# Encoder trunk with two attention mixers: the amount of filler between attention rounds corrected in 28 of 218 rounds, filler allowed past four group ends, ten attention steps moved by a round or by some places

## The chip, the cores and the metric

One Trainium2 chip, one of its cores. The metric is device time in microseconds (us) of one execution of the whole program, the median over repeated runs. The core has five instruction queues that matter here: TensorE (PE, with PEld for its weight loads), VectorE (DVE), ScalarE (ACT), GpSimd (POOL), and SyncE (SP), which only issues DMA transfers.

## The reference

One transformer layer on 1,280 tokens of width 1,024 (1,024 of one request group, 256 of another), all in float32:

```python
n = _rms_norm(h, g_mix, NORM_EPS)
z = jnp.einsum('bsd,dc->bsc', n, w_in)
qa, ka, va, qb, kb, vb = jnp.split(z, cuts, axis=-1)
# mixer A: 4 heads, two softmax maps per head, distance penalty
sc = jnp.einsum('bqhcd,bkhcd->bhcqk', qb, k) * scale - slopes * dist
pr = jax.nn.softmax(sc, axis=-1)
out = jnp.einsum('bhqk,bkhe->bqhe', pr[:, :, 0] - lam * pr[:, :, 1], v)
# mixer B: 8 query heads on 2 key/value heads, normed and rotated q and k
ob = _gqa_attention(qb, kb, vb)
h = h + jnp.einsum('bsc,cd->bsd', jnp.concatenate([oa, ob], -1), w_out)
a = jax.nn.relu(jnp.einsum('bsd,df->bsf', _rms_norm(h, ...), w_ff1))
h = h + jnp.einsum('bsf,fd->bsd', a * a, w_ff2)
h = h + sigmoid(_rms_norm(h, ...) @ w_ple_gate) * (p @ w_ple_proj)
return _rms_norm(h, g_final, NORM_EPS)
```

The softmax is exact: the maximum over the keys is taken, then the exponential, then the division by the sum.

## The kernel before

Every float32 matrix product is made of three matmuls of rounded parts: high by high, high by low, low by high. So nearly every operand is split first: ACT copies it to the rounded type (the high part), and DVE or POOL subtracts that from the original (the low part).

**Stages.** Up to about 120 us the tokens are normed and projected to the B mixer's q, k, v and the A mixer's v. Then the A mixer's q and k follow, and the attention of all heads starts at about 197 us and runs to about 711 us, with other matmuls woven between its steps. Behind it come the rest of the output projection, the transposes of the normed tokens, the MLP (seven products in place of eight, from about 790 us), the gate and the last norm. The change touches the attention stage alone.

**Attention units.** A unit is one head (or one of the two heads of a B pair) on 256 queries, against 1,024 or 256 keys. There are 60 units, written X here as A0 to A3 and B4 to B7 with the number of the first 128-token block: "B7 at block 6, first head". Their work is cut into steps, and each step is put down for a *round* by `at(r, ph, fn)`: `r` is the round, `ph` the phase within it, `fn` records the instructions. The steps of a unit are:

- `qk`: the scores, four matmuls of 512 columns into the PSUM tile `sc` (two buffers), L671;
- `mx`: the row maximum on DVE, with the distance penalty for A (L684, 1,024 columns), without it for B (L688);
- `ex`: the exponential on ACT (L693 for A, L696 for B); for B it is what frees the `sc` buffer, for A `mx` is;
- `cb`: the division, on POOL, and for A the difference of the two maps on DVE (L706);
- `tr`, `hi`, `lo`: four transposes on PE into the PSUM tile `tr` (two buffers, L725), the high part `ph` on ACT (L731), the low part `pl` on DVE (L736), which frees the `tr` buffer;
- `av`: the product with the values, two matmuls with `ph` (four for A) and two with `pl` (L749), two rounds after the `tr`; at the end of an A unit the norm of its result (L763 to L783, with a matmul L768 of the squares `osq`).

A unit with 1,024 keys has four `tr` steps in four rounds, and the next unit's `tr` steps follow; its scores stand four to seven rounds earlier. There are 218 rounds, 0 to 217.

**Filler.** Between the phases of a round the loop takes work from a generator, `side_work`. It holds first the q and k projections of A heads 1 to 3 (`psa`, L284), then, once the input activations are no more needed, the output projection: a first half for all ten token tiles (channels 0, 1, 4, 5), then the second half. Each token tile has two groups of twelve 512-column matmuls, `pso`. The generator hands out three matmuls at a time and says what they cost in the planner's units (648 for three of 512 columns); at the end of a group it says 0.0. How much is taken is a debt, `owed`:

```python
owed += max((cost + lead) * (0.0 if r <= 6 else RATIO if r < LATE else RATIO2), LEAD.get(r, 0.0))
while owed > 0:
    d = next(side, None)
    if op_done and not WN[0]:
        w1_fetch(0, 1)
    norms()
    if not d:
        owed = 0.0
        break
    owed -= d
```

`cost` is the planned cost of the round's attention matmuls, and 500 more is added for each `av` step of the round; `RATIO` is 0.43, and 0.6 from round 160 on. So at a group's end the round takes nothing more, and what is left of the debt is dropped. The evacuation of a finished group is recorded at the next round's start. Some of the 0.0 stand for preparation alone: when the output projection opens, each of four of them splits one channel's weights (`ow`: ACT L914, POOL L915) after their DMA has landed.

What the rounds do not take is left to a loop behind the attention, which alternates the remaining `pso` groups with the token transposes `trn` (L1137).

**What sets the order.** The recorded order is a priority. A scheduler then lists each engine's instructions, so matmuls of one step can stand between those of another; each engine then runs its own list in order. The places below are shown as that final list.

Of the kernel before, what the change touches and what calls it, by code (L numbers as in the profile page):

```python
# [46 lines left out]
def encoder_kernel(ctx: ExitStack, tc: tile.TileContext, x, xT, pT, w_in, w_out, w_ff1, w_ff2, w_gate, w_proj,  # L47
                   g_mix, g_mlp, g_ple, g_subln, g_final, g_qn, g_kn, lams, rope, dist, y):
    nc = tc.nc
    pp2 = []  # L50
    LEAD = {4: 2000., 5: 2000., 6: 2000.}
    PRE = 14000
    Y = (0, 1, 1)
# [52 lines left out]
    dp = ctx.enter_context(tc.tile_pool(name="dram", bufs=1, space=DRAM))  # L106
# [462 lines left out]
    def flush():  # L569
        todo, deferred[:] = deferred[:], []  # L570
        for fn in todo:
            fn()
# [33 lines left out]
    rounds = collections.defaultdict(list)  # L606
    PH = {n: i for i, n in enumerate(("ld", "tr", "mx", "hi", "ex", "cb", "st", "lo", "qk", "fill", "av", "fin"))}

    def at(r, ph, fn):
        rounds[r].append((PH[ph], len(rounds[r]), fn))  # L610

    def mixed_out(r, ch, t0, get):

        st = {}

        def hi():
            st["hl"] = tl("ml")
            S.activation(st["hl"][:, 0], get(), AF.Copy)

        def lo():  # L620
            hl = st["hl"]
            G.tensor_tensor(hl[:, 1], get(), f(hl[:, 0]), op=ALU.subtract)
            dma(MD[ch][:, :, t0:t0 + 256], f(hl[:]))
            md_done[ch, t0] = True

        at(r, "fin", hi)
        at(r + 1, "fin", lo)

    def plan_unit(kind, idx, t0, c, b, shared):
# [26 lines left out]
        def values():  # L656
# [3 lines left out]
            st["v"] = vals[n]  # L660

        at(when[0] - 3, "ld", start)
        at(when[0], "st", values)

# [336 lines left out]
    def w1_fetch(p, i):  # L1001
        hl = slot(f"W{EARLY[p][i]}", [P, 2, 4, P], F32R, "w1")
        dma(f(hl[:]), wed[p, i])
        WN[p][i] = hl[:, 0], hl[:, 1]
# [47 lines left out]
    def norms():  # L1052
        nonlocal normed
        while normed < len(op_done):
            mlp_norm(op_done[normed])
            normed += 1
# [4 lines left out]
    owed = PRE  # L1061
    while owed > 0:
        d = next(side)
        flush()
        owed -= d
    owed = 0.0
    last = max(rounds)
    for r in range(min(rounds), last + 1):
        cost = 0.0
        todo = sorted(rounds[r], key=lambda q: q[:2])  # L1070
        for ph, _, fn in todo:
            if ph < PH["fill"]:
                cost += fn() or 0.0
        flush()
        lead = sum((fn_ph == PH["av"]) * LC for fn_ph, _, _ in todo)
        owed += max((cost + lead) * (0.0 if r <= 6 else RATIO if r < LATE else RATIO2), LEAD.get(r, 0.0))
        while owed > 0:
            d = next(side, None)
            if op_done and not WN[0]:
                w1_fetch(0, 1)  # L1080
            norms()
            if not d:
                owed = 0.0
                break
            owed -= d
        for ph, _, fn in todo:
            if ph >= PH["fill"]:
                fn()
# [788 lines left out]
```

## Time and profile before

| | |
|---|---|
| median of the runs | 1680.98 us (1680.25 to 1682.56, three runs) |
| the profiled execution | 1681.47 us |
| its span, first to last instruction | 1679.7 us |
| granted TensorE clock, mean over the span | 0.997 of full speed |
| matmuls in the span | 9,777 |

The profiled execution is 0.49 us over the median, and 1.8 us of it lie outside the span. In the rows below "idle before" is time in which the engine had nothing running ahead of that instruction, and the arrow names what it waited for.

### The profile page before, as it was taken

How to read it: one execution, taken by the hardware profiler on the slowest of the kernel's cores; microseconds unless marked ns; L12 is line 12 of the kernel's file. 1: busy time of each engine (PE TensorE's matmuls, PEld its weight loads, DVE VectorE, ACT ScalarE, POOL GpSimd, SP SyncE). 2: the span in 40 equal slices, each digit the busy share in tenths (PEclk: the TensorE clock that was granted, in tenths of full speed). 3: DMA queues.
4: the chain of work that ended last, by engine and by line, in shares of the span. 5: the costliest groups of instructions: out<-in, count | busy, mean ns of one | idle time of the engine just before them, and what ended most of it. 6: DMA issues, size and time to landing. Idle time of an engine off the chain costs nothing.

```text
span 1679.7 us, 27298 instructions
## 1 busy us (share of the span) xinstructions
PE 1638.0 (98%) x9777; PEld 1468.3 (87%) x9777; DVE 1207.8 (72%) x2130; ACT 882.4 (53%) x1717; POOL 668.8 (40%) x706
## 2 busy tenths in 40 slices
PE   8999999999899999999999999999999999999997
PEld 8999888888788888889999999999888888888885
DVE  7788588778788878668766666666664856855876
ACT  8544377776776667675333332333433435745534
POOL 1123455545654445333656556630533400003343
PEclk9999999999999999999999999999999999999998
DMA  9766853432963434396433434439776459980463
GB/s 313 238 216 230 250 154 108 132 108 94 261 185 122 138 91 130 109 309 203 158 123 130 159 129 137 135 126 390 239 228 201 159 188 358 334 290 15 158 212 107
DMA packets 205964, 309.22 MB, mean 184 GB/s; under 512 B 14714, under 2 KB 124932, under 8 KB 205828
## 3 DMA queue, kind: packets, MB, share of 16 engines
q1 hardware_dynamic: 203940, 301.96, 54.9%
q0 software_dynamic: 1600, 5.24, 1.0%
q8 instruction: 77, 1.26, 0.3%
q14 instruction: 59, 0.48, 0.1%
q10 hardware_dynamic: 288, 0.27, 0.0%
HBM read 200.45 MB, written 101.72 MB: 180 GB/s over the span
## 4 chain that ended last, share of the span: by engine, by line
PE 81%; DVE 6%; DMA 5%; issue 3%; ACT 3%; POOL 2%; SPq 1%; POOLq 0%; ACTq 0%; DVEq 0%
PE psa L284 6%; PE sc L671 6%; PE av L749 5%; PE psg L1696 4%; PE tr L725 4%; PE pso L284 4%; PE psb L284 3%; PE psv L284 2%; PE psp L176 1%; DMA xt<-in_x 1%; DVE pl L736 1%; DMA h_sb<-in_x 1%; PE f__15611 L176 1%; DVE mm L688 1%; DVE nlo L1232 1%
## 5 line engine op out<-in xcount | busy, mean ns | idle before, releaser
L671 PE MATMUL sc<-kt,qt 128*128 128x512 f32 (+1 forms) x576 | 156.2, 391 | 8.3 <-ACT p L696 6.0
L736 DVE TENSOR_TENSOR pl<-tr,ph 128x512 fp32r<-128x512 f32 x204 | 138.0, 684 | 32.1 <-ACT ph L731 30.5
L731 ACT ACTIVATE ph<-tr 128x512 fp32r<-128x512 f32 x204 | 119.8, 595 | 56.8 <-PE tr L725 50.1
L1411 DVE TENSOR_TENSOR ao<-ar,ao 128x1280 fp32r<-128x1280 f32 x56 | 96.6, 1726 | 68.3 <-ACT ao L1409 68.3
L1409 ACT ACTIVATE ao<-ar 128x1280 fp32r<-128x1280 f32 x56 | 71.0, 1270 | 128.7 <-PE f__14937 L176 31.6
L284 PE MATMUL pso<-ow,mt 128*128 128x512 f32 x480 | 119.3, 395 | 3.0 <-DVE osq L776 1.3
L671 PEld LDWEIGHTS sc<-kt,qt 128*128 128x128 f32 x576 | 98.7, 188 | 26.8 <-ACT p L696 7.5
L725 PE MATMUL tr<-ident,p 128*128 128x128 f32 x768 | 115.6, 273 | 6.4 <-DVE pl L736 5.7
L725 PEld LDWEIGHTS tr<-ident,p 128*128 128x128 f32 x768 | 91.3, 140 | 23.0 <-DVE pl L736 9.3
L1125 POOL TENSOR_SCALAR w1r<-w1r,gmlp 128x256 f32<-128x256 f32 x112 | 79.1, 724 | 67.3 <-DMA w1r<-in_w_ff 67.3
L284 PEld LDWEIGHTS pso<-ow,mt 128*128 128x128 f32 x480 | 87.4, 188 | 21.1 <-DVE osq L776 2.0
L749 PE MATMUL av<-ph,vt 128*128 128x256 f32 x544 | 101.7, 288 | 0.8 <-DVE osq L776 0.4
L1198 ACT ACTIVATE w<-w1s 128x512 fp32r<-128x512 f32 x56 | 35.2, 629 | 114.7 <-POOL w1s L1205 55.1
L710 POOL TENSOR_SCALAR p<-p,rl 128x1024 f32<-128x1024 f32 x64 | 74.9, 1171 | 50.8 <-DVE rl L708 47.4
L1696 PE MATMUL psg<-gbo,gao 128*128 128x512 f32 (+1 forms) x387 | 91.0, 385 | 0.0
L688 DVE TENSOR_REDUCE mm<-sc 128x1 f32<-128x1024 f32 (+1 forms) x80 | 84.2, 1056 | 8.9 <-PE sc L671 8.4
L749 PE MATMUL av<-pl,vt 128*128 128x256 f32 x408 | 89.1, 300 | 0.0
L1798 POOL TENSOR_TENSOR ra<-ra 128x512 f32<-128x512 f32 x5 | 7.1, 1429 | 204.9 <-DVE gao L1542 204.9
L749 PEld LDWEIGHTS av<-ph,vt 128*128 128x128 f32 x544 | 81.8, 188 | 6.3 <-DVE osq L776 1.0
L696 ACT ACTIVATE p<-sc,mm 128x1024 f32<-128x1024 f32 x64 | 71.3, 1115 | 25.4 <-DVE mm L688 16.7
L1696 PEld LDWEIGHTS psg<-gbo,gao 128*128 128x128 f32 x387 | 70.9, 188 | 14.6
L684 DVE CUSTOM_DVE_ANT_0 p<-sc,dist 128x1024 f32<-128x1024 f32 x64 | 77.6, 1218 | 7.8 <-PE sc L671 3.8
(1545 smaller groups left out, 4829.1 us busy)
## 6 DMA issues: line engine op xcount, KB each, us to landing
ar<-ad SPq DMA_DIRECT2D x56, 640.0 KB, 5.2
w2r<-in_w_ff SPq DMA_DIRECT2D x56, 512.0 KB, 4.9
qt<-qd SPq DMA_DIRECT2D x160, 128.0 KB, 3.0
ad<-q SPq DMA_DIRECT2D x64, 320.0 KB, 2.9
ad<-qs SPq DMA_DIRECT2D x48, 320.0 KB, 2.2
w1r<-in_w_ff SPq DMA_DIRECT2D x28, 512.0 KB, 4.2
md<-ml SPq DMA_DIRECT2D x40, 256.0 KB, 2.5
mt<-md SPq DMA_DIRECT2D x20, 512.0 KB, 6.0
```

What stands on the lines that cost most here:

```text
L284: PE.matmul(ps, a, b, start=i == 0, stop=i == n - 1)
L671: PE.matmul(ps[:, h0:h0 + n], shared["q"][:, cc, v, i * P:(i + 1) * P], kt[:, s0 + h0:s0 + h0 + n], start=v == 0, stop=v == 1)
L684: V.tensor_tensor_reduce(out=p[:, :sn], in0=ps[:, :sn], in1=dst_t[:, off:off + sn], scale=SLOPES[idx], scalar=3.0e38, op0=ALU.add, op1=ALU ...
L688: V.tensor_reduce(out=st["m", i][:, 0:1], in_=ps[:, :sn], axis=AX.X, op=ALU.max, negate=True)
L710: G.tensor_scalar(p[:, :sn], p[:, :sn], rl[:, 0:1], 1.0, op0=ALU.mult, op1=ALU.mult)
L725: PE.transpose(t[:, jj, i * P:(i + 1) * P], st["ws"][i][:, j * P:(j + 1) * P], ident)
L731: S.activation(ph, st["tr", j2], AF.Copy)
L736: V.tensor_tensor(pl, st["tr", j2], f(st["ph", j2][:]), op=ALU.subtract)
L749: PE.matmul(st["av"][:, :256], x_, y_, start=j2 == 0 and n == 0, stop=j2 == nj - 1 and n == len(pr) - 1)
L1125: G.tensor_scalar(raw[:, k], raw[:, k], gmlp[:, 4 * kh + k:4 * kh + k + 1], 1.0, op0=ALU.mult, op1=ALU.mult)
L1411: V.tensor_tensor(ao[:, 1], a, f(ao[:, 0]), op=ALU.subtract)
L1696: ends[:] = [PE.matmul(ps, a, w, start=n == 0, stop=n == len(pr) - 1)]
```

## The change

```diff
+    FIX = {49: -1320, 59: -660, 62: 660, 66: -660, 75: -660, 76: 330, 79: 660, 81: 2000, 82: 660, 83: -660,
+           84: 660, 104: -1000, 106: -1320, 109: -1000, 116: -660, 118: 660, 122: -660, 130: 660, 140: -660, 146: -330,
+           150: -330, 169: 1320, 173: -330, 174: -1320, 188: -660, 189: 660, 206: 660, 209: -660}
+    BRK = {43: 2, 106: 1, 191: 1, 205: 2}
+    MV = {50: (0, -10), 109: (1, 0), 264: (-1, 0), 637: (0, -2), 1178: (-1, 0), 1275: (1, 0), 1291: (0, 10), 1491: (-1, 0),
+          1546: (0, -2), 1681: (0, 2)}
+    n_at = itertools.count()
...
     def at(r, ph, fn):
-        rounds[r].append((PH[ph], len(rounds[r]), fn))
+        dr, dp = MV.get(next(n_at), (0, 0))
+        rounds[r + dr].append((PH[ph], len(rounds[r + dr]) + dp, fn))
...
         owed += max((cost + lead) * (0.0 if r <= 6 else RATIO if r < LATE else RATIO2), LEAD.get(r, 0.0))
+        owed += FIX.get(r, 0.0)
+        brk = BRK.get(r, 0)
         while owed > 0:
...
             if not d:
+                if d is not None and brk > 0:
+                    brk -= 1
+                    flush()
+                    continue
                 owed = 0.0
                 break
```

`FIX` adds to or takes from the debt of 28 rounds; 660 is about one portion of three 512-column matmuls. `BRK` lets four rounds go on past a group's end, one or two times. `MV` moves ten of the steps: by a round (first number) or by places within the phase (second).

Followed round by round, the tables do less than they list. In rounds 43, 106 and 205 the loop meets no group end (in 43 and 106 the debt is below zero), so only round 191 goes past one. The added debt of rounds 169 and 189 is dropped at a group end. The moves 50 and 264 leave every engine's list as it was, and move 109 only lets SP issue the four query loads of B4 at block 8 ahead of the four of B4 at block 2, some 200 us into the program. PE's list is the same up to its matmul 2,228 (at 321 us in the trace), and DVE's, ACT's and POOL's up to about the same time. From there on the amount of filler behind the old one runs like this: 648 to 1,944 units less through rounds 49 to 80, up to 1,944 more in rounds 81 to 101, then less again, 1,296 at round 109, 2,592 at 122, 3,888 at 148, 6,480 at 175, and 7,776 from round 197 on. So 36 `pso` matmuls (three groups) come behind the last `av` that stood before it. The opening of the output projection, which had rounds 103 to 107 without matmuls of filler, now has rounds 102 to 109 without any. Nothing is added or removed: 576 `psa`, 480 `pso` and all attention matmuls remain, as do all instructions of the other engines. SP issues the same transfers, and where its list differs one to four neighbours change places; the loads of the residual rows and of `mt`, which belong to the filler, fall some places later along with their groups.

Three places on PE, with what stood there and what stands there now. In all three, `tr` rows of four are one `tr` step; `pso` is filler.

The first is near the end of the attention, with the `tr` steps of B7 at block 6, first head (four) and A3 at block 6 (four). Before:

```order
L725 MATMUL tr<-ident,p 128x128 x4
L749 MATMUL av<-pl,vt_8146 128x256 x2
L725 MATMUL tr<-ident,p 128x128 x9
L284 MATMUL pso<-ow,mt 128x512 x12
L725 MATMUL tr<-ident,p 128x128 x7
```

Now:

```order
L733 MATMUL tr<-ident,p 128x128 x4
L757 MATMUL av<-pl,vt_8111 128x256 x2
L733 MATMUL tr<-ident,p 128x128 x4
L291 MATMUL pso<-ow,mt 128x512 x12
L733 MATMUL tr<-ident,p 128x128 x4
L776 MATMUL av<-osq,mean_m 128x256
L733 MATMUL tr<-ident,p 128x128
```

The first row is the second `tr` step of B7, and the nine held its third, its fourth and one matmul of A3's first. The filler group now stands between the third and the fourth. A little further on, A3's third and fourth `tr` steps stood right behind the `av` rows of B7; the list there was

```order
L768 MATMUL av<-osq,mean_m 128x256
L725 MATMUL tr<-ident,p 128x128 x8
L284 MATMUL pso<-ow,mt 128x512 x12
L725 MATMUL tr<-ident,p 128x128 x8
L749 MATMUL av<-ph,vt_8146 128x256 x4
```

and is now

```order
L757 MATMUL av<-pl,vt_6362 128x256 x2
L291 MATMUL pso<-ow,mt 128x512 x12
L733 MATMUL tr<-ident,p 128x128 x8
L291 MATMUL pso<-ow,mt 128x512 x12
L757 MATMUL av<-ph,vt_8111 128x256 x4
```

so that a filler group has come ahead of them.

The second place is in the B6 unit at block 2, first head: its second `tr` step, then its third and fourth together. Ahead of them stand two groups of scores of A2 at block 2; the score behind them is the first of B6 at block 4, and it takes the buffer of the first of those two. Before:

```order
L671 MATMUL sc<-kt,qt 128x512 x4
L749 MATMUL av<-ph,vt_6357 128x256 x2
L671 MATMUL sc<-kt,qt 128x512 x4
L725 MATMUL tr<-ident,p 128x128 x4
L749 MATMUL av<-pl,vt_6357 128x256 x2
L768 MATMUL av<-osq,mean_m 128x256
L725 MATMUL tr<-ident,p 128x128 x8
L671 MATMUL sc<-kt,qt 128x512 x4
L725 MATMUL tr<-ident,p 128x128 x4
L284 MATMUL pso<-ow,mt 128x512 x12
```

Now:

```order
L679 MATMUL sc<-kt,qt 128x512 x4
L733 MATMUL tr<-ident,p 128x128 x4
L757 MATMUL av<-pl,vt_6362 128x256 x2
L776 MATMUL av<-osq,mean_m 128x256
L679 MATMUL sc<-kt,qt 128x512 x4
L733 MATMUL tr<-ident,p 128x128 x8
L291 MATMUL pso<-ow,mt 128x512 x12
L679 MATMUL sc<-kt,qt 128x512 x4
```

The second A2 group has moved between the `tr` steps, and the filler group ahead of B6's score.

The third place is the last unit, B7 at block 6, second head: its third and fourth `tr` steps and the `av` that need them. Before:

```order
L725 MATMUL tr<-ident,p 128x128 x8
L768 MATMUL av<-osq,mean_m 128x256
L749 MATMUL av<-ph,vt_6357 128x256 x2
L749 MATMUL av<-pl,vt_6357 128x256 x2
L749 MATMUL av<-ph,vt_6357 128x256 x2
L749 MATMUL av<-pl,vt_6357 128x256 x2
L749 MATMUL av<-ph,vt_6357 128x256 x2
L749 MATMUL av<-pl,vt_6357 128x256 x2
L749 MATMUL av<-ph,vt_6357 128x256 x2
L749 MATMUL av<-pl,vt_6357 128x256 x2
```

Now, from the fourth `tr` step on:

```order
L733 MATMUL tr<-ident,p 128x128 x4
L757 MATMUL av<-pl,vt_6362 128x256 x2
L757 MATMUL av<-ph,vt_6362 128x256 x2
L757 MATMUL av<-pl,vt_6362 128x256 x2
L757 MATMUL av<-ph,vt_6362 128x256 x2
L757 MATMUL av<-pl,vt_6362 128x256 x2
L1151 MATMUL trn<-ident,h_sb 128x128 x4
```

The last two `av` rows need the `ph` and the `pl` of that fourth step. Seven rows lay between it and the first of them, and three lie there now.

## The prediction

> **What bounds the kernel now.** First the page's busy times, then the same by stage.
>
> ```profile
> span 1679.7 us, 27298 instructions
> PE 1638.0 (98%) x9777; PEld 1468.3 (87%) x9777; DVE 1207.8 (72%) x2130; ACT 882.4 (53%) x1717; POOL 668.8 (40%) x706
> ```
>
> ```profile
> core 0: us, PE busy (x) PEld busy (x) DVE busy (x) ACT busy (x) POOL busy (x), PEclk, DMA share, GB/s
> ...
> 120.00:320.00 200.00, 198.52 (x1273) 177.45 (x1272) 158.55 (x339) 118.48 (x257) 99.08 (x104) 1.00 0.60 182
> 320.00:720.00 400.00, 381.61 (x2365) 330.31 (x2365) 312.12 (x588) 278.27 (x582) 199.50 (x217) 1.00 0.46 136
> 720.00:790.00 70.00, 67.15 (x394) 60.62 (x393) 53.18 (x105) 45.05 (x90) 22.37 (x31) 1.00 0.80 262
> ```
>
> PE is the bound, and the change neither adds nor removes a matmul. So the time can change only by PE's idle time: 400 - 381.61 = 18.4 us in the stretch from 320 to 720 us, where the lists differ, and 2.9 us behind it. DVE has 312 us of work there, 78%: it is no bound on the average, but in a stretch of some microseconds it may be. Next, who is waited for there:
>
> ```profile
> line engine op names shapes xcount | busy us, mean ns | idle before us <-releasers
> L671 PE MATMUL sc<-kt,qt 128*128 128x512 f32 (+1 forms) x420 | 113.6, 391 | 8.3 <-ACT p L696 6.0 <-DVE mm L684 1.9
> L736 DVE TENSOR_TENSOR pl<-tr,ph 128x512 fp32r<-128x512 f32 x159 | 108.0, 685 | 27.8 <-ACT ph L731 26.5 <-PE av L768 0.3
> L731 ACT ACTIVATE ph<-tr 128x512 fp32r<-128x512 f32 x158 | 93.1, 595 | 46.2 <-PE tr L725 40.8 <-PE av L749 4.6
> L284 PE MATMUL pso<-ow,mt 128*128 128x512 f32 x357 | 90.0, 395 | 3.0 <-DVE osq L776 1.3 <-DVE o L797 0.7 <-ACT ow L914 0.5
> L725 PE MATMUL tr<-ident,p 128*128 128x128 f32 x592 | 88.6, 273 | 6.3 <-DVE pl L736 5.7 <-DVE rl L703 0.4
> L749 PE MATMUL av<-ph,vt 128*128 128x256 f32 x426 | 79.2, 287 | 0.8 <-DVE osq L776 0.4 <-ACT ph L731 0.2
> ```
>
> The idle time before PE's groups (8.3 + 3.0 + 6.3 + 0.8) makes up the 18.4 us. Almost all of it is a wait for a PSUM buffer: `sc` until ACT or DVE has read it, `tr` until `pl` is made. Both have two buffers. So what counts at each place is the **distance**: how much other PE work stands between the group that fills a buffer and the one that wants it back. PE's pace for that work, from the chain of waits:
>
> ```profile
> 418.79 1.86 PE sc L671 x8
> 421.36 0.44 PE tr L725 x4
> 501.44 1.88 PE av L749 x16
> 586.81 2.77 PE pso L284 x12
> ```
>
> A `tr` step is 0.44 us, a score group of four 0.93, a pair of `av` 0.235, a whole filler group 2.77. The single waits, from the timeline of PE:
>
> ```profile
> 369.97 0.66 PE L725 MATMUL tr<-ident,p 128*128 128x128 f32 x4 [0.75 <-DVE pl L736]
> 371.11 1.21 PE L671 MATMUL sc<-kt,qt 128*128 128x512 f32 x4 [0.48 <-DVE mm L684]
> 408.96 0.65 PE L725 MATMUL tr<-ident,p 128*128 128x128 f32 x4 [1.14 <-DVE pl L736]
> 446.50 1.20 PE L671 MATMUL sc<-kt,qt 128*128 128x512 f32 x4 [2.93 <-ACT p L696]
> 460.23 0.51 PE L284 MATMUL pso<-ow,mt 128*128 128x512 f32 x1 [0.54 <-ACT ow L914]
> 461.59 0.73 PE L284 MATMUL pso<-ow,mt 128*128 128x512 f32 x2 [0.42 <-POOL ow L915]
> 494.00 0.60 PE L725 MATMUL tr<-ident,p 128*128 128x128 f32 x4
> 495.23 0.66 PE L725 MATMUL tr<-ident,p 128*128 128x128 f32 x4 [0.63 <-DVE pl L736]
> 496.37 1.20 PE L671 MATMUL sc<-kt,qt 128*128 128x512 f32 x4 [0.48 <-DVE mm L684]
> 535.87 3.02 PE L284 MATMUL pso<-ow,mt 128*128 128x512 f32 x12 [0.66 <-DVE o L797]
> 622.06 3.06 PE L284 MATMUL pso<-ow,mt 128*128 128x512 f32 x12 [1.34 <-DVE osq L776]
> 643.62 1.19 PE L671 MATMUL sc<-kt,qt 128*128 128x512 f32 x4 [1.08 <-ACT p L696]
> 688.52 1.05 PE L725 MATMUL tr<-ident,p 128*128 128x128 f32 x5 [1.11 <-DVE pl L736]
> 696.77 1.45 PE L725 MATMUL tr<-ident,p 128*128 128x128 f32 x8 [0.77 <-DVE pl L736]
> ```
>
> **The change, part by part.** The sum is made against the profiled execution, 1681.47 us, which lies 0.49 us over the median.
>
> *The end, 686 to 699 us.* The fourth `tr` step of B7 wants the buffer of the second; between them stood a pair of `av` and the third step, 0.235 + 0.44 = 0.67 us. The trace shows what is needed there:
>
> ```profile
> 686.14 0.60 PE L725 MATMUL tr<-ident,p 128*128 128x128 f32 x4
> ```
>
> That is the second step; its PE time ends at 686.14 + 0.44 = 686.58, and the fourth starts at 688.52, 1.94 us later. Now a filler group stands between as well, and the distance is 0.67 + 2.77 = 3.44 us. The wait of 1.11 goes. The 0.77 at 696.77 goes too: the same `pl` gets another 2.77 us. What is late next is nothing with less than about 2 us, until the last unit (below). Term: -1.9.
>
> *B6 at block 2, 493 to 497 us.* The fourth step has 0.235 + 0.24 + 0.44, some 0.9 us, behind the second, and 0.93 more now: 1.8 against the 1.9 needed (the trace's L768 row is taken as a pair of `av`). The 0.63 shrinks to about 0.1. The next score wanted a buffer left 0.24 + 0.93 + 0.44 + 0.48 + 0.88 = 3.0 us earlier and waited 0.48; now it is 0.44 + 0.48 + 0.93 + 0.88 + 2.77 = 5.5 us. Term: -0.9.
>
> *370 us (B5 at block 2).* The list shows the same: `tr` steps three and four had 1.14 and 0.9 us behind them and have 5.0 and 2.0, by the same pace. The two rows hold 1.23 us, and both distances end above 1.94: -1.2.
>
> *643.62.* The score's buffer was left 0.7 us of `pso`, 0.93 of scores and 0.88 of `tr` earlier, 2.5 in all; now it is 6.7. But the exponential that frees it stands on ACT behind a split that waits for weights:
>
> ```profile
> 641.84 0.63 ACT L914 ACTIVATE ow<-h_sb 128x512 fp32r<-128x512 f32 x1 [0.99 <-DMA h_sb<-in_w_out]
> ```
>
> Those splits come with the filler, and move some rounds later with it, where they can block another exponential. I take -0.7 of 1.08; the bounds are -1.1 and +1.
>
> *The opening of the output projection, 440 to 462 us.* ACT is the queue here:
>
> ```profile
> 444.19 0.63 ACT L914 ACTIVATE ow<-h_sb 128x512 fp32r<-128x512 f32 x1 [1.16 <-DMA h_sb<-in_w_out]
> 444.84 0.38 ACT L796 ACTIVATE osq<-av 64x256 f32<-64x256 f32 x1
> 445.25 1.11 ACT L696 ACTIVATE p<-sc,mm 128x1024 f32<-128x1024 f32 x1
> ```
>
> The score at 446.50 waits for this `p`. In the new list ACT runs the same weight split ahead of it, but `osq` behind it: 0.4 us earlier. The transfers are issued at the same point of PE's list, so they land as before; the wait stays, at about 2.5. The first `pso` come later (seven of them behind the A1 `av`, where four stood ahead), so the 0.54 and 0.42 for the fourth channel's weights should mostly go. Term: -1.1, bounds -2 and, if ACT's blocked queue holds the new eight rounds without filler longer, +2.
>
> *Some eight more waits, the 0.66 at 535.87 the largest*, at 345 to 350, 527 to 540 and 652 to 656 us, stand where the list now has more PE work between. The waits shown one by one add up to 12.3 of the 18.4 us; I count this 0.66 and 2.2 of the 6.1 that the group rows hold beyond them to these places. Half of 2.9 goes: -1.4.
>
> *408.96, 622.06 and one of 0.7 at 478 us* (from the 6.1), 3.2 us in all: the distances change, but DVE's list ahead of the awaited instruction does too. Nothing to choose by; 0, bounds -3.2 and +3.2.
>
> *New waits.* Filler given to one place is missing at another. In the last unit the third and fourth `tr` steps stood together, with seven `av` rows (1.6 us) ahead of the first `av` that needs the fourth; three rows (0.7 us) are left, and to the `pl` row 0.94. The trace's nearest row has 1.87 us there and PE still waits a little ahead of it:
>
> ```profile
> 710.20 0.39 PE L749 MATMUL av<-ph,vt 128*128 128x256 f32 x2
> 710.60 0.50 PE L749 MATMUL av<-pl,vt 128*128 128x256 f32 x2
> ```
>
> (0.4 us from one start to the next, in place of 0.235.) So about 2.0 is needed and 0.94 is there: +1.1, and nothing hides it but the 0.4 us of `trn` behind, which PE reaches only afterwards. Four `tr` steps get distances of 1.3 to 1.6 us where 1.94 is needed: B7 at block 2 (1.34), B5 at block 2 (1.37), B6 and B7 at block 4 (1.58 each); 0.6 + 0.6 + 0.4 + 0.4 = +2.0. The rest of the list has a few distances near the limit: +0.5. Together +3.6; bounds +1 and +8.
>
> *Restarts.* A score group behind a wait shows 1.20 us (446.50), an undisturbed one 0.93 and a last 0.16 of drain: some 0.1 us more for each wait. About nine waits fewer: -0.9.
>
> *Moved steps.* The two later exponentials and transposes that move do so by one round, among rows with slack; the query loads that change places are issued by
>
> ```profile
> 203.55 7.97 SPq L598 DMA_DIRECT2D qt<-qd  x8
> 223.21 1.10 PE L671 MATMUL sc<-kt,qt 128*128 128x512 f32 x4
> ```
>
> 211.5 us, and the first score that uses them starts at 223.2; a landing takes some microseconds and is covered either way. Without that cover it would cost what landing exceeds. The 36 `pso` that come behind the attention fill a stretch in which PE has 2.9 of 70 us idle: 0, between -1 and +1.
>
> Sum: -1.9 - 0.9 - 1.2 - 0.7 - 1.1 - 1.4 + 3.6 - 0.9 = -4.5; with a little from the tail, -5. 1681.47 - 5 = 1676.5 for a profiled execution, **1676.0** on the median's scale.
>
> **One rule of the skill.** In every stretch quoted PEclk is 1.00, the one with the 2.93 us wait too. The Trainium skill (TensorE: Matmul & The Clock Gate, section HAM oscillation — how this bites in real kernels) warns of idle gaps of PE over about 3.4 us, behind which the clock is halved for a while; by that rule, too, the longest gap here is harmless, and the trace agrees.
>
> **Rivals.** *The waits only change places*: DVE's 312 us are the same, filler covers one place by uncovering another, and new waits eat what old ones give. Speaks for it: DVE at 78%. Against: the largest single distances clearly grow. New waits at 6.5 in place of 3.6 give -2: 1679.
>
> *Most waits go*: if the corrected rounds fit the true pace of ACT and DVE, 13 of 18.4 us go and 3 come: 1671, or 1668 with restarts.
>
> *Thinned cover, slower*: 36 x 0.23 = 8.2 us of matmuls leave rounds 109 to 197 for the time behind the attention, where they cover nothing. This decides where a run of `tr` steps has more DVE work than PE work; then PE idles for what was taken. If two thirds of 8.2 come back as waits (5.5) on top of the 3.6, against gains of 6.1: 1681 + 3 = 1684.
>
> *A long idle at the opening*: eight rounds without filler in place of five. If the 2.93 grew by 0.5 us and the clock fell for as long a stretch, 3.4 us of matmuls would take twice as long: 1676 + 0.5 + 3.4 = 1680. This is what the page named above would make of it; nothing in the trace has come so far.
>
> *That the tables do nothing* can be excluded: PE's list differs from its matmul 2,228 on.
>
> **How the numbers follow.** Forecast 0.47 (1672 to 1679), waits change places 0.25 (1677 to 1681), most waits go 0.15 (1666 to 1672), thinned cover 0.11 (1682 to 1688), clock 0.02. The range is 1667 to 1682. A difference of 0.2%, 3.4 us, is about what a measurement can tell from none: faster than 1677.6 is most of the forecast and the whole third case, 0.58; same 0.31; slower 0.11.
>
> **What would show it.** Right: idle from 320 to 720 us of 13 to 14 us; no wait at the last filler groups before the end; a wait of about 1 us before the last `av`; the large wait at the opening at about 2.5. Wrong: idle unchanged with other names, or new waits over 1 us on `tr` at B6 and B7, block 4; or the opening's wait above 3 us; or a tail from 710 us on with more idle than now.

## The result, and the profile after

| | before | after |
|---|---|---|
| median of six runs each | 1681.54 us | 1672.93 us |
| ratio, with its 95% interval | | 0.9948 (0.9937 to 0.996) |
| the profiled execution | 1681.47 us | 1672.21 us |
| its span | 1679.7 us | 1670.1 us |

The kernel is 8.6 us faster, 0.52%. The page after, its first lines:

```profile
span 1670.1 us, 27285 instructions
PE 1637.6 (98%) x9777; PEld 1473.1 (88%) x9777; DVE 1206.4 (72%) x2130; ACT 880.8 (53%) x1717; POOL 668.8 (40%) x706
```

PE does the same work in the same busy time, 1637.6 us against 1638.0. The gain is PE's idle time, less what two stretches at half clock cost, which the page counts as busy (last section). By stage (stretch, its length, then the busy time of each engine, granted clock, share of the DMA engines, rate):

```profile
320.00:720.00 400.00, 389.50 (x2417) 341.33 (x2418) 321.30 (x604) 282.88 (x594) 203.25 (x221) 1.00 0.49 148
720.00:790.00 70.00, 67.79 (x410) 62.94 (x409) 52.45 (x98) 42.39 (x82) 20.61 (x31) 0.98 0.68 229
```

In the stretch where the lists differ, 18.4 us of idle time became 10.5. The groups of the same stretch (busy, mean, and idle time before them with what ended it):

```profile
L679 PE MATMUL sc<-kt,qt 128*128 128x512 f32 (+1 forms) x420 | 112.1, 392 | 4.6 <-ACT p L704 2.9 <-DVE mm L692 1.5
L291 PE MATMUL pso<-ow,mt 128*128 128x512 f32 x393 | 98.8, 396 | 2.3 <-DVE osq L784 1.3 <-POOL ow L923 0.8
L733 PE MATMUL tr<-ident,p 128*128 128x128 f32 x592 | 88.4, 274 | 2.8 <-DVE pl L744 2.6
L757 PE MATMUL av<-ph,vt 128*128 128x256 f32 x426 | 80.3, 290 | 1.6 <-DVE h_sb L981 0.7 <-DVE o L805 0.6
```

Scores wait 4.6 us in place of 8.3, `tr` 2.8 in place of 6.3, filler 2.3 in place of 3.0; `av` wait 1.6 in place of 0.8. The single waits, from the timeline of PE:

```profile
368.98 0.63 PE L733 MATMUL tr<-ident,p 128*128 128x128 f32 x4 [1.70 <-DVE pl L744]
374.16 0.51 PE L757 MATMUL av<-ph,vt 128*128 128x256 f32 x2 [0.63 <-DVE o L805]
442.05 1.21 PE L679 MATMUL sc<-kt,qt 128*128 128x512 f32 x4 [1.98 <-ACT p L704]
458.31 0.74 PE L291 MATMUL pso<-ow,mt 128*128 128x512 f32 x2 [0.82 <-POOL ow L923]
471.13 0.66 PE L733 MATMUL tr<-ident,p 128*128 128x128 f32 x4 [0.75 <-DVE pl L744]
487.88 0.66 PE L733 MATMUL tr<-ident,p 128*128 128x128 f32 x4 [0.17 <-DVE pl L744]
489.88 1.21 PE L291 MATMUL pso<-ow,mt 128*128 128x512 f32 x4 [1.34 <-DVE osq L784]
527.29 0.50 PE L757 MATMUL av<-ph,vt 128*128 128x256 f32 x2 [0.72 <-DVE h_sb L981]
610.24 1.20 PE L679 MATMUL sc<-kt,qt 128*128 128x512 f32 x4 [0.37 <-DVE mm L692]
674.12 0.60 PE L733 MATMUL tr<-ident,p 128*128 128x128 f32 x4
692.23 0.51 PE L757 MATMUL av<-pl,vt 128*128 128x256 f32 x2 [0.22 <-DVE pl L744]
```

Of the thirteen waits shown for before, three have a wait left at the same place (442.05, 458.31, 487.88). The row at 674.12 is the fourth `tr` step of B7 at block 6, which waited 1.11 us before. But others are new, those at 368.98 and 489.88 the largest.

To compare lists in which filler stands in different places, I add up, along PE's list, what each matmul's start is later than the one before plus that one's pace (227 ns for 512 columns, 117 for 256, 109 for 128). Up to the last `av`, the sum is 48.2 us before and 38.0 after; to the last matmul of the program 58.4 and 49.3. So the attention gained 10.2 us, and 1.1 us came back behind it (the last section says from where). 0.4 us of the gain lie ahead of the first difference in PE's list. That much is chance: up to there the ten traces of the experiments below lie between 1.7 us under and 1.5 us over the sum of before, with one and the same list.

### The profile page after: what moved, and what is told of

Its sections match the earlier page's. It is cut to its first block, busy times and chain, and to the rows that moved or that the text cites. A ratio compares the mean times of both kernels' runs of the same rounds, so it can differ in the third digit from the quotient of the medians.

```text
span 1670.1 us, 27285 instructions
## 1 busy us (share of the span) xinstructions
PE 1637.6 (98%) x9777; PEld 1473.1 (88%) x9777; DVE 1206.4 (72%) x2130; ACT 880.8 (53%) x1717; POOL 668.8 (40%) x706
## 4 chain that ended last, share of the span: by engine, by line
PE 74%; DVE 8%; issue 6%; DMA 5%; ACT 3%; POOL 3%; SPq 1%; DVEq 0%; POOLq 0%; ACTq 0%
PE psa L291 7%; PE sc L679 6%; PE av L757 5%; PE psg L1710 4%; PE pso L291 4%; PE tr L733 4%; PE psb L291 3%; PE psv L291 2%; DMA w2r<-in_w_ff 2%; PE psp L183 1%; POOL kt L1431 1%; DVE wo L1426 1%; DVE pl L744 1%; DVE p L692 1%; DMA h_sb<-in_x 1%
```

## The experiments

All ratios are to the kernel before, runs of the same chip beside them. The first time named for an experiment is the median of its runs; gains and losses in us are worked out from the ratio, which can differ from the quotient of the two medians by up to 0.0006. The diffs are shortened: `...` stands for numbers that stay. From e7 on `BRK` is empty, and `MV` holds the one move of e5 or, in e7, none.

| | left of the change | ratio | 95% interval |
|---|---|---|---|
| e1 | corrections of rounds 49 to 84 | 0.9966 | 0.9953 to 0.9979 |
| e2 | corrections of rounds 104 to 209, group ends | 1.0045 | 1.0032 to 1.0058 |
| e3 | all 28 corrections | 0.9966 | 0.9954 to 0.9979 |
| e4 | moved steps and group ends | 1.0001 | 0.9993 to 1.001 |
| e5 | all corrections, one moved step | 0.9937 | 0.9924 to 0.9951 |
| e6 | e2's corrections, one in place of the early eleven, moved steps | 0.9976 | 0.9965 to 0.9986 |
| e7 | all corrections, three rounds late | 1.0024 | 1.0011 to 1.0037 |
| e8 | e5, the opening's three corrections as one | 0.9941 | 0.9928 to 0.9954 |
| e9 | rounds 173 to 209, one entry ahead, one move | 1.0009 | 1.0 to 1.0018 |
| e10 | rounds 146 to 209, another entry ahead, one move | 0.9979 | 0.997 to 0.9988 |

**e1, the early half.**

```diff
-    FIX = {49: -1320, ..., 84: 660, 104: -1000, ..., 209: -660}
+    FIX = {49: -1320, ..., 84: 660}
+    BRK = {}
+    MV = {}
```

> The corrections of rounds 49 to 84 alone (nine other corrections, the group end of 191 and the moved steps left out). TensorE's list is that of the change up to its matmul 3,005 (about 446 us) and 36 matmuls of filler do not come behind the attention here: the last av stands where it stood before. Theory of distances: what the change gained up to that point stays, about 3.2 us by the two traces' sums of idle time at the last av of B5 at block 6, and the rest is as before: 3 us faster than before, 2 to 4. Rival, the gain is that less filler is left in the attention: no gain, 0. Rival, any other order gives another time by chance: anything within 5 us on either side, with no trace of it at 346, 370 and 409 us.

1676.17 us, 0.9966: 5.7 us faster, more than the 2 to 4 expected. (Seventeen corrections are left out; the nine in the expectation is a miscount.) The sum of idle time up to the `av` of B5 at block 6 was 3.7 us lower than before, near the 3.2 foreseen, and 0.6 of it lie ahead of the first difference; a further 1.9 came at 520 to 546 us, since the amount of filler that the early half leaves behind still shifts the list there. No filler beyond that of before comes behind the attention. So two thirds of the gain come without any less filler in the attention.

**e2, the late half.**

```diff
-    FIX = {49: -1320, ..., 104: -1000, ..., 209: -660}
+    FIX = {104: -1000, ..., 209: -660}
-    MV = {...}
+    MV = {}
```

> The corrections of rounds 104 to 209 and the group end of 191 alone, no moved step. TensorE's list is that of before up to its matmul 2,993 (about 447 us); 24 matmuls of filler come behind the attention in place of 36. Theory of distances: the waits of before at 370, 409 and 446 us come back, those at 495, 622, 643, 688 and 697 go, where the distances are now 1.8, 1.8, 9.5, 6.0 and 3.9 us (as long as in the change or longer): 6 us faster than before, 4.5 to 7.5. Together with the early half it makes up the whole, within 1.5 us. Rival of less filler in the attention: two thirds of the whole gain of 8.6, 5.7 us, which here is the same; the early half tells them apart.

1689.91 us, 1.0045 (1.0032 to 1.0058): **8 us slower than before** where 6 faster was expected. This is the run on which the theory of the prediction fell. Its groups from 320 to 720 us:

```profile
L676 PE MATMUL sc<-kt,qt 128*128 128x512 f32 (+1 forms) x420 | 113.7, 393 | 11.6 <-DVE mm L689 5.3 <-ACT p L701 5.2 <-ACT pq L701 1.0
L730 PE MATMUL tr<-ident,p 128*128 128x128 f32 x596 | 88.8, 274 | 4.2 <-DVE pl L741 3.7 <-DVE rl L708 0.4
L288 PE MATMUL pso<-ow,mt 128*128 128x512 f32 x338 | 86.0, 399 | 2.8 <-DMA mt<-md 2.3 <-DVE o L802 0.5
```

The longer distances did for `tr` what they should: its waits fell from 6.3 us to 4.2. But the scores' rose from 8.3 to 11.6, and 2.3 us of waiting for a transfer came to the filler. From matmul 2,228, where the list of the whole change leaves that of before, to the last `av`, PE's idle time is 2.5 us more than before. Of the rest of the profiled execution's 8.3 us, two stretches at half clock, from 674.1 and 769.7 us on, cost some 1.7 us each, and 1.5 us lie ahead of any difference. The rows:

```profile
535.29 1.21 PE L676 MATMUL sc<-kt,qt 128*128 128x512 f32 x4 [1.84 <-ACT p L701]
620.22 1.65 PE L676 MATMUL sc<-kt,qt 128*128 128x512 f32 x6 [2.15 <-DVE mm L689]
656.82 1.65 PE L676 MATMUL sc<-kt,qt 128*128 128x512 f32 x5 [1.41 <-DVE mm L689]
673.43 1.92 PE L288 MATMUL pso<-ow,mt 128*128 128x512 f32 x5 [2.29 <-DMA mt<-md]
```

The first two of these scores lost PE work ahead of them: by the same pace as above, 3.65 and 5.64 us lay between the fill of the buffer and the score in the kernel before, 1.78 and 2.92 lie there now. The third did not. It is the score at 655.82 of before, which has 1.78 us there and waits 0.30; here it has 2.01 us and waits 1.41.

**e3, the corrections alone.**

```diff
-    BRK = {43: 2, 106: 1, 191: 1, 205: 2}
-    MV = {...}
+    BRK = {}
+    MV = {}
```

> All 28 corrections, no round past a group end, no moved step. TensorE's list is that of the change up to its matmul 3,467 (about 516 us) and ends with the same 36 matmuls of filler behind the attention. Theory of distances: one place near the end, the third tr step of A3 at block 6, has 1.14 us of work behind the fill of its buffer in place of 3.39, so a wait of about 1 us is there; else the change: 7 us faster than before, 6 to 8.5. Rival, the moved steps or the group end of 191 carry a good part: 5 us or less.

1676.62 us, 0.9966: 5.7 us faster, between the two marks and 3 us behind the change (3.7 between the medians; the two intervals overlap a little). The wait expected at A3's third `tr` step was 0.45 us, but another came, for the first filler of the second half:

```profile
657.73 1.62 PE L288 MATMUL pso<-ow,mt 128*128 128x512 f32 x6 [1.33 <-DMA mt<-md]
```

SP issues that `mt` at 652.23; PE wants it 4.2 us later and has it 5.5 us later. A second wait, 1.15 us for the `osq` of A3 at block 4, stands at 673.68.

**e4, the moved steps and group ends alone.**

```diff
-    FIX = {...}
+    FIX = {}
```

> The ten moved steps and the four entries for group ends, with none of the 28 corrections. TensorE's list is that of before up to its matmul 3,129 (about 473 us). Theory of distances: of the places with a wait only the score of B6 at block 4 (496 us) gets a longer one, 2.9 us to 4.7, and its 0.5 to 0.65 us go: 0.5 us faster, 0 to 1.5, which the measurement can hardly tell from none. Rival, the moved steps carry a good part of the gain: 3 us or more.

1682.22 us, 1.0001 (0.9993 to 1.001): nothing, as expected.

**e5, one move.** e3 says that moves are worth some 3 us, e4 that they are worth nothing; both can hold if they are worth something only with the corrections' filler around them. Of the ten, one alters PE's list after its matmul 3,583.

```diff
-    BRK = {43: 2, 106: 1, 191: 1, 205: 2}
-    MV = {50: ..., 1681: (0, 2)}
+    BRK = {}
+    MV = {1491: (-1, 0)}
```

> All 28 corrections and of the ten moved steps only one: the third tr of A3 at block 2 goes from round 185 to 184. No group end is passed. TensorE's list is that of the change but for 36 matmuls from its 3,467 to its 3,582, where it is that of the run with the corrections alone. Theory now (a wait is set by what the lists hold around it, and the move is worth what it makes of the filler behind it): the time of the change, 8 to 9 us faster than before, so 3.7 us faster than with the corrections alone; the waits of 1.3 us for mt at 658 us and of 1.2 us at 674 us are gone. Rival, the other moves carry these 3.7 us: 5 us faster than before, as with the corrections alone.

1672.75 us, 0.9937 (0.9924 to 0.9951): the whole gain. At the place where e3 waited, the timeline now has

```profile
657.41 2.21 PE L288 MATMUL pso<-ow,mt 128*128 128x512 f32 x9
```

without a wait; `mt` is issued at 651.59, and PE comes for it 5.8 us later. The wait at 673.68 is gone as well; the two made up 2.5 us in e3. The step that is moved, a `tr` of A3 at block 2, runs at 629 us, 28 us ahead of this. What it does is in the loop: `cost` of round 184 grows by that step and that of 185 falls, the filler taken shifts, and the second half's first group comes a little later behind its load. With the moved steps in place, the entry for round 191 leaves every engine's list as it is; it did nothing.

**e6, the late half with one entry ahead.**

```diff
-    FIX = {49: -1320, ..., 84: 660, 104: -1000, ...}
+    FIX = {81: 1010, 104: -1000, ...}
-    BRK = {43: 2, 106: 1, 191: 1, 205: 2}
+    BRK = {}
```

> The late half again (corrections of rounds 104 to 209), with the moved steps, without the entries for group ends, and with one correction ahead of it in place of the twelve early ones: 1,010 units more at round 81, which is their sum. From its matmul 3,233 on TensorE's list is that of the change, and up to 2,587 that of before. Theory now: the late corrections are neither good nor bad; they fit if the filler ahead of them has the right amount, so that its groups fall where they fell in the change. The waits of before at 346, 350 and 370 us stay, all others are those of the change: 7 us faster than before, 5.5 to 8. Rival, each correction has its own worth, and the worths add: the late ones cost 8 us and one small entry can't turn that: 5 to 8 us slower than before.

The early corrections that the one entry stands for are eleven, not twelve. 1678.8 us, 0.9976: 4 us faster, short of the 5.5 to 8 expected, but on the other side of e2, which was 8 slower with the same late corrections. From matmul 3,233 on PE's list is the change's, and the idle sum from the `av` of B6 at block 2 to the last one grew by 5.6 us less than it does before; in the change it is 6.5. The rest is what its own list had ahead of it, between 2,587 and 3,233: a wait of 2.05 us at a score at 409.5 us, and seven of 0.2 to 1.1 us from 459 to 476.

**e7, the same numbers three rounds later.**

```diff
-    FIX = {49: -1320, 59: -660, 62: 660, ...}
+    FIX = {52: -1320, 62: -660, 65: 660, ...}
```

> The same 28 numbers, each three rounds later (52 to 212), no moved step, no group end passed. 24 matmuls of filler come behind the attention, and at the places with the largest waits of before the tr buffers get distances as long as in the change (5.0, 2.1, 1.8, 2.7 and 6.0 us; only one, A3 at block 6, falls to 1.1). Theory of my prediction (distances of tr decide): 5 to 8 us faster than before. Rival, less filler in the attention decides: 5.7 faster. Theory now: scores, DVE's queue and the transfers of mt must fit as well, and nothing here fits them: less than half of the change's gain, between 4 us faster and 6 slower.

1687.14 us, 1.0024 (1.0011 to 1.0037): 4 us slower, though 24 matmuls went behind the attention and no `tr` of those places but one had a short distance. Both older theories forecast 5 us or more of gain. In the profiled execution the attention's idle time did not fall (0.8 us more than before, counted as for e2); the larger part of the loss lies behind it, with waits of 2.21 and 2.49 us and 6.8 us at half clock.

**e8, the opening.**

```diff
+    FIX = {..., 111: -3320, ...}
-    FIX = {..., 104: -1000, 106: -1320, 109: -1000, ...}
```

> The run with one move, but the three corrections of the opening (rounds 104, 106 and 109) are taken out, and their sum, 3,320 units less, is put at round 111. So the first pso stand at matmul 3,005 as with the early half alone, 24 places earlier than in the change, and TensorE's list differs from that of the run with one move in the 49 matmuls from 3,005 to 3,096 alone (about 447 to 462 us). Theory now: the big wait there, 1.8 to 2.1 us at the score of B6, belongs to the weights' transfers and stays; the three corrections are worth nothing of their own but their sum: within 1.5 us of the run with one move, so 8 to 11 us faster than before. My prediction's term (a later opening lets the waits of 0.54 and 0.42 us for the weights go): 1 us slower than the run with one move, and waits for ow at the first pso groups.

1673.35 us, 0.9941 (0.9928 to 0.9954), as e5: 10 us faster. The score at the opening waits as it did:

```profile
440.85 1.34 PE L676 MATMUL sc<-kt,qt 128*128 128x512 f32 x4 [1.94 <-ACT p L701]
```

**e9, the end alone.**

```diff
+    FIX = {160: -5280, 173: -330, 174: -1320, 188: -660, 189: 660, 206: 660, 209: -660}
+    MV = {1491: (-1, 0)}
```

> Corrections of rounds 173 to 209 and the one moved step alone, and one entry of 5,280 units less at round 160, so that the same 36 matmuls of filler come behind the attention. TensorE's list is that of before up to its matmul 3,769 (about 575 us), and from 4,207 on nearly that of the change. Theory now: the waits of before at 643 (1.2 us), 652 to 656 (0.9), 688 (1.3) and 697 us (1.3) go, half a microsecond to one comes new: 4 us faster than before, 2.5 to 5.5. Rival, the late corrections are of use only behind the early ones, as the late half seemed to say: no gain or slower.

1683.5 us, 1.0009 (1.0 to 1.0018): no gain, where 2.5 to 5.5 us were expected. The waits at 643, 688 and 697 us went, and waits of 0.69 and 0.55 us at 650 us and of 0.63 at 685 came, and the one of e2:

```profile
605.85 2.89 PE L288 MATMUL pso<-ow,mt 128*128 128x512 f32 x12
609.96 0.86 PE L676 MATMUL sc<-kt,qt 128*128 128x512 f32 x3
614.55 1.09 PE L730 MATMUL tr<-ident,p 128*128 128x128 f32 x8
617.80 1.65 PE L676 MATMUL sc<-kt,qt 128*128 128x512 f32 x6 [2.15 <-DVE mm L689]
```

Read what DVE did, which frees that score's buffer with the `mm` of 616.51 (L689):

```profile
613.82 0.17 DVE L708 RECIPROCAL rl<-ll 128x2 f32<-128x2 f32 x1 [1.12 <-ACT p L698]
614.02 0.21 DVE L710 TENSOR_SCALAR rl<-rl,neglam 128x1 f32<-128x1 f32 x1
614.24 0.69 DVE L741 TENSOR_TENSOR pl<-tr,ph 128x512 fp32r<-128x512 f32 x1
615.31 1.29 DVE L711 SCALAR_TENSOR_TENSOR p<-p,rl 128x1024 f32<-128x1024 f32 x1 [0.38 <-POOL p L709]
616.51 1.22 DVE L689 CUSTOM_DVE_ANT_0 p<-sc,dist 128x1024 f32<-128x1024 f32 x1
```

The `mm` stands in DVE's list behind the division of another A map, which needs ACT's exponential (1.12 us of waiting), then POOL (0.38), and takes 1.29 us itself. The buffer that the score wants was filled by 612.4, four microseconds before that `mm` starts; DVE reads it late because its own queue waits.

**e10, the end with its groups in their places.** As e9, with the entry ahead chosen so that PE's list is that of before up to matmul 3,519 and the change's from 3,583 on.

```diff
-    FIX = {160: -5280, 173: -330, ...}
+    FIX = {143: -3240, 146: -330, 150: -330, 169: 1320, 173: -330, ...}
```

> As the run with the end alone, but with the corrections from round 146 on (146, 150, 169, 173, 174, 188, 189, 206, 209), the one moved step, and one entry of 3,240 units less at round 143 in place of the 5,280 at round 160. The same 36 matmuls of filler come behind the attention. TensorE's list is that of before up to its matmul 3,519 (about 537 us) and that of the change from 3,583 on; what differs from the run with the end alone is where the groups of filler stand between 3,519 and 4,206. Theory now: with the groups where the change has them, the wait of 2.3 us at the score of B7 at block 4 (618 us) is not there and the end gains what it gained in the change, 4.5 us by the sums of idle time from the last av of B6 at block 6 to the last av of all: 4.5 us faster than before, 3 to 6. Rival, the late corrections are worth nothing without the early ones whatever the groups' places, or moving 36 matmuls behind the attention costs what the end gains: within 1.5 us of before, as the run with the end alone.

1678.63 us, 0.9979 (0.997 to 0.9988): 3.5 us faster. As many matmuls of filler come behind the attention as in e9, and the list is nearly the same from 4,207 on. The same score and the DVE rows ahead of it:

```profile
606.20 2.21 PE L288 MATMUL pso<-ow,mt 128*128 128x512 f32 x9
608.25 1.08 PE L676 MATMUL sc<-kt,qt 128*128 128x512 f32 x4
616.31 1.21 PE L676 MATMUL sc<-kt,qt 128*128 128x512 f32 x4 [0.37 <-DVE mm L689]
```

```profile
611.98 0.17 DVE L708 RECIPROCAL rl<-ll 128x2 f32<-128x2 f32 x1 [0.76 <-ACT p L698]
612.18 0.21 DVE L710 TENSOR_SCALAR rl<-rl,neglam 128x1 f32<-128x1 f32 x1
612.40 1.29 DVE L741 TENSOR_TENSOR pl<-tr,ph 128x512 fp32r<-128x512 f32 x2
613.60 1.28 DVE L711 SCALAR_TENSOR_TENSOR p<-p,rl 128x1024 f32<-128x1024 f32 x1
615.02 1.23 DVE L689 CUSTOM_DVE_ANT_0 p<-sc,dist 128x1024 f32<-128x1024 f32 x1
```

Between the fill of that buffer and the score that wants it stand 2.5 us of PE work, less than e9's 2.9, and it waits 0.37 us in place of 2.15. What differs ahead of it is, above all, the second score group of A3 at block 2's first half (the row at 608.25; in e9 the one at 609.96, which ends it): it stands within the filler here and behind it in e9. So the chain that it starts begins earlier, DVE's reciprocal at 611.98 in place of 613.82, and `p` doesn't wait for POOL. With e1 (5.7) the halves add up to 9.2 us, the change's 8.7 within the intervals, once each has its groups where they fit. The traces agree: by 545 us the sum of e1 is 6.1 us below that of before and the change's 5.9; from there to the last `av` e10 gains 3.6 us and the change 4.3.

## Why the prediction was right, and where it was not

The forecast was 5 us faster, the measurement 8.6; the direction, the range and the bound were right. The size was not: the measured time lies nearer to the rival "most waits go" (13 us go, 3 come, 1671) than to the forecast's 1676. Several terms were off in both directions, so that the sum came out as near as it did is in part luck. By its own steps:

- **PE's idle time is all that can change.** Nearly right: busy time is the same within 0.4 us, but it holds two stretches at half clock that before does not have. They cost some 1.5 us at the opening and 1.8 behind the attention (last section), each about half of the 3.4 that the rival on the clock reckoned with. The prediction gave a fall of the clock a chance of 0.02 and no place in the sum, since before's longest wait, 2.93 us, had passed without one.
- **The end, 686 to 699** (-1.9): right. Neither wait is left; the 674.12 row is one of the two places.
- **B6 at block 2** (-0.9): right at its two rows, 0.63 to 0.17 and 0.48 to none. But the filler behind it now waits 1.34 us for `osq` (489.88), which the sum didn't have there.
- **370 us** (-1.2): the two rows went, and the step after them got 1.70 (368.98). Its distance had even grown, from 1.3 to 1.8 us; DVE's queue was late, as the rows in the last part show.
- **643.62** (-0.7): the whole 1.08 went.
- **The opening** (-1.1): 3.9 us of waits became 2.8, the right number from the wrong parts. The score's wait was to fall by 0.4 us and fell by 0.95; the waits for `ow` were to go for the most part and fell by 0.14. The traces of the other runs part the two causes of the score's wait. ACT waits for the weights' landing first, in the change and in e1, which has the same list there:

```profile
440.27 0.63 ACT L922 ACTIVATE ow<-h_sb 128x512 fp32r<-128x512 f32 x1 [0.56 <-DMA h_sb<-in_w_out]
441.24 0.63 ACT L919 ACTIVATE ow<-h_sb 128x512 fp32r<-128x512 f32 x1 [1.42 <-DMA h_sb<-in_w_out]
443.01 1.21 PE L676 MATMUL sc<-kt,qt 128*128 128x512 f32 x4 [2.81 <-ACT p L701]
```

  The last row is e1's score; the change's waits 1.98. With this list ACT waits 0.26, 0.50, 0.56, 0.66 and 1.42 us in e5, e8, the change, e3 and e1, and the score 1.65, 1.94, 1.98, 2.07 and 2.81: always 1.4 us more. With the list of before the score waits 1.65, 1.66 and 1.70 us in e4, e10 and e2, where ACT has no wait for the weights, and 2.25 and 2.93 in e9 and before, where it has 0.48 and 1.16. So the new list is worth 0.25 to 0.4 us, about as forecast, and the rest of the fall is that the weights happened to land sooner. e8 shows that the corrections of the opening are worth only their sum.
- **Eight smaller waits** (half of 2.9, -1.4), **408.96, 622.06 and 478** (0 for 3.2): mis-sized. Of the former all went, of the latter 1.14 and 1.34 did and 0.75 stayed: -2.9 and -2.4. These two terms are 3.9 us more gain than forecast.
- **New waits** (+3.6): wrong in place, and 1.4 us too small in sum. At the last `av` 0.22 us came in place of 1.1, at the four `tr` steps with 1.3 to 1.6 us 0.2 at most; at rows that were not named 1.70, 1.34, 0.72, 0.63 and 0.37, some 5 together. For the four `tr` steps the limit of 1.94 us was the error: it was measured as elapsed time and held against pure PE work. Between the fill of their buffers and the steps themselves 2.0 to 2.5 us elapsed in the change. At the step of B7 at block 2 (work of 1.34 us between) it was 2.0, with the wait of 0.37 us at 610.24 among them.
- **Restarts** (-0.9): mis-sized. From the first difference in PE's list to the last `av`, the waits over 0.15 us fell from 29 to 14, where nine fewer were reckoned with; and from start to start each costs some 0.16 us more than its row shows (1.87 us at the row of 1.70). That is some -2.4.
- **Moved steps** (0): as hidden work, right (e4); but one of them decides where filler falls, and without the moves (e3) the change loses a third of its gain, which that one brings back (e5). The forecast did not see that since it read the final list only.

Of the signs named ahead, one came, no wait at the last filler groups; idle time was 10.5 us and not 13 to 14, and the waits at the opening (1.98) and before the last `av` (0.22) were smaller than named.

The step that failed as a principle is **"what counts at each place is the distance"**. e2, e7 and e9 give the `tr` steps that waited in before distances near the change's or longer, wherever they alter the list there (one apart, in e7), and these waits go; yet the kernels gain nothing or lose. Other waits come, and some of them against the distance: the score of e2 at 656.82, and in the change the step at 368.98. The trace of before held a warning too: its `tr` step at 408.96 has 4.1 us of work behind the fill of its buffer and waits 1.14. A buffer comes free at the end of a chain that runs through ACT, POOL and DVE, each in its own order; where a long instruction or a wait stands in one of these queues, the same distance is too short (e9 against e10). The rival "thinned cover" priced a cause that is real: in e2 and e9 work is missing ahead of scores, which wait 1.84 (e2) and 2.15 us (both). In the change itself, it did not come. That the gain is simply the smaller amount of filler in the attention is excluded by e1 (none moved behind, 5.7 us gained) and e9 (36 moved behind, no gain).

What stays open: why ACT waits up to 1.2 us more or less for the weights at the opening with one list, and whether yet other tables would take away the 1.70, 1.98 and 1.34 us that are left. The chain through DVE was read from e9 against e10, which differ at that place in several rows; no run moved the one score group alone. e5 and e8 are as fast as the change, with fewer entries; no run was clearly faster than it.

## What to carry to other kernels

Filler that is dealt out by a running debt and in whole groups has a memory: a correction shifts all groups behind it, so that the same late corrections stand in a kernel 8 us slower than before and, with one entry ahead of them, in one 4 us faster. Test such tables as a whole, and after cutting one in parts compare the final lists, not the entries. And when asking whether a buffer will be free, follow the chain that frees it through each engine's own list, with the long instructions and the waits in it; the work that PE has meanwhile says only half.

## What the runs showed of the hardware

**The clock can fall behind a wait of 2 us.** Behind the attention, a matmul waits 1.94 us for the normed tokens, from 751.28 to 753.22. The change's profile, in stretches of 1 us (busy time of each engine, clock third from the end):

```profile
753.00:754.00 1.00, 0.78 (x4) 0.78 (x5) 1.00 (x2) 1.00 (x3) 0.00 (x0) 1.00 0.06 25
754.00:755.00 1.00, 1.00 (x6) 1.00 (x5) 1.00 (x1) 1.00 (x3) 0.00 (x0) 0.56 0.03 12
755.00:756.00 1.00, 1.00 (x6) 0.90 (x5) 1.00 (x2) 1.00 (x3) 0.00 (x0) 0.50 0.00 0
757.00:758.00 1.00, 1.00 (x5) 1.00 (x5) 1.00 (x3) 0.91 (x2) 0.00 (x0) 0.73 0.00 0
```

The clock is halved for 3.4 us, beginning 0.9 us after the wait has ended. The same happened behind the 1.98 us at 442.05, from 443.5 on; there e5, with the same list and no drop, loses 1.5 us less. From 753.22 to 758.71 PE runs eight matmuls of 384 columns, eight transposes and eight more such matmuls; at before's pace (1.39 us for eight of the former, 0.9 of the latter) they take 3.7 us, so some 1.8 us are lost. With the wait itself that is 3.7 us where before has waits of 1.01, 0.39 and 0.92 us: 1.4 more, which accounts for what came back behind the attention. Yet e5, whose list differs in 36 matmuls far from both places, waits 1.65 and 2.29 us there and stays at 1.00, and so does before behind 2.93 us.

What decides it can be read from the traces' clock records. In all twelve, every stretch at one clock but the last lasts a whole number of times 3.413 us; so the clock changes only at the bounds of windows of that length, and these begin at another point in each run (the first bound lies 7.8 to 11.3 us into the span). Counting in each window the time in which no matmul runs, one finds:

| run | wait ends at | its length | idle time of the fullest window | clock behind that window |
|---|---|---|---|---|
| before | 446.50 | 2.93 us | 1.61 us | 1.00 |
| e1 | 443.01 | 2.81 us | 1.67 us | 1.00 |
| e5 | 752.6 | 2.29 us | 1.66 us | 1.00 |
| after | 442.05 | 1.98 us | 1.95 us | 0.50 |
| after | 753.22 | 1.94 us | 1.94 us | 0.50 |
| e8 | 440.85 | 1.94 us | 1.94 us | 0.50 |

Up to 1,600 us the twelve traces hold 5,598 windows. Fourteen are followed by half clock, and each of these has 1.89 us of idle time or more; none of the others has more than 1.70. (Behind 1,650 us, at the end of the program, three windows with 1.80 to 1.93 were not followed by a drop.) So a wait of 2.9 us that a bound cuts in two was harmless, and one of 1.94 inside a window was not; since the bounds lie elsewhere in each execution, the list alone does not say which it will be. The Trainium skill (TensorE: Matmul & The Clock Gate, section HAM oscillation — how this bites in real kernels) sets the limit at gaps of about 3.4 us; here a gap of 1.94 us was enough, and the measurement decides. The same page of the Trainium skill (section Part 1: The HAM clock gate) says that the clock is set by a free-running window of activity and that its effect varies from run to run; the traces agree, as the records above show.

**An instruction of DVE can take nearly twice its time.** The division of the A maps, 1,024 columns, over the whole attention of the change (minimum, median and maximum in ns):

```profile
L714 DVE SCALAR_TENSOR_TENSOR p<-p,rl x32: 1269/1376/2332, 222.8 to 674.9; 128x1024 f32<-128x1024 f32 x32
```

The longest is the one behind the new wait at 368.98, on DVE and on POOL:

```profile
365.90 2.33 DVE L714 SCALAR_TENSOR_TENSOR p<-p,rl 128x1024 f32<-128x1024 f32 x1
368.15 0.68 DVE L744 TENSOR_TENSOR pl<-tr,ph 128x512 fp32r<-128x512 f32 x1
```

```profile
365.86 1.29 POOL L869 TENSOR_TENSOR zl<-zl 128x512 fp32r<-128x512 f32 x1 [0.62 <-ACT zl L868]
```

In the two traces of before and after, every one with nothing of POOL beside it took 1.27 to 1.29 us, and every one over 1.5 us had POOL at work beside it, though some beside POOL took 1.27 as well. All twelve traces together, 384 of these instructions, show the same. It was seen and not tried.
